# Norm roots on GpSimd, later GLA and MLA pieces, and keys and values loaded by block in a hybrid GLA/MLA layer

## The chip, the cores and the metric

The kernel runs on one core of one Trainium2 chip. The metric is the device time of one execution in microseconds (us), the median of several runs. The core has a tensor engine (PE, with its weight loads PEld), a vector engine (DVE), a scalar engine (ACT), a GpSimd engine (POOL) and a sync engine (SP) that here issues nearly all DMAs. Each engine runs its instructions in the order in which they stand in its queue.

## The reference, cut to what matters

One layer on x of shape (1, 2048, 1024) in float32:

```
n   = rms_norm(x, attn_norm);  z = n @ w_in     # split into gq gk gv g_low g_r c_q c_kv k_r
GLA: log_a = log_sigmoid(g_low @ w2 + b) / 16;  b = cumsum(log_a) in a chunk
     o_g   = chunked linear attention with exact pairwise decays (4 heads, 64 keys, 128 values)
     o_g   = rms_norm(o_g per head, gla_out_norm) * silu(g_r)
MLA: q = rms_norm(rms_norm(c_q) @ w_uq per head), k = rms_norm([rms_norm(c_kv) @ w_ukv, k_r] per head)
     rope on the last 32 of 96 dimensions;  o_m = block-causal softmax attention (8 heads)
h = x + concat(o_g, o_m) @ w_out
h = h + relu(rms_norm(h) @ w_up)^2 @ w_down
h = h + (p @ w_ple_proj) * sigmoid(rms_norm(h) @ w_ple_gate + b_ple_gate)
```

Every `rms_norm` needs the reciprocal root 1/sqrt(mean of squares + eps), one number a row (x, h), four a row (GLA heads) or eight a row (four query and four key heads).

## The kernel before

The work stands in three stages that follow each other.

The **first stage** (about 0 to 690 us) takes four blocks of 512 rows. For each block the rows of x are normed (`norm_rows`) and transposed into `nT`; then come the products with slices of `w_in`, each as three matmuls on a split into a high and a low part (`mm3`, lines 99 to 101): columns for c_q, g_low and k_r (304 wide), c_kv and a part of gv (320), gq and gk, the rest of gv (320), g_r (256). Each weight slice is split by ACT and DVE (lines 95, 96). Between these products two queues of small pieces are drained one by one by calls in the loops: `pend` holds the GLA pieces of the block before (`gla_pieces`: a diagonal, seven decay levels, the decays, two chunks, for each of two units of 256 rows), `mla_q` holds the MLA tiles (`mla_tile`: eight a block, each with its two products, norm, scaling, and a `store` that transposes q and k and writes them to DRAM). `later` holds a piece's second half back by one piece.

The **second stage** (to about 1260 us) is attention over eight heads and four query blocks; the last block's GLA pieces are drained inside it. The **third stage** (to the end) is the output product, the MLP and the gate, in two halves of 1024 rows; `rows_T` norms and transposes there.

The order on each engine is set by the framework's scheduler, which sorts the recorded instructions by priority (the order of the code) and its own cost estimates; loads of the activation table are put in afterwards where the functions demand them.

Lines that the prediction speaks of: `rstd_of` (106 to 115) makes the root: v on DVE (106), a first guess by an Exp on ACT (108), three Newton steps of three DVE instructions each (111, 112, 114). Line 428 transposes a GLA chunk's output `o`, which line 422 scales by the root; line 354 transposes the decayed keys `dk` (347). Lines 617 to 630 make the log decays `la` (Abs, Exp, Ln on ACT) and their running sums `bt` (matmul by a triangle, line 628). Line 384 is a level's score product, which needs `xq` and `dl` (377, 379) and those an Exp (368). Line 499 scales q by its root and gains, 501 and 503 scale k; line 511 transposes both. Line 740 sets a row of the key buffer `kT` to one. Line 921 transposes the normed h of the third stage.

Of the kernel before, what the change touches and what calls it, by code (L numbers as in the profile page):

```python
# [48 lines left out]
def hymba_block(ctx, tc, x, p, positions, attn_norm, w_in, gla_gate_w2, gla_gate_b,  # L49
# [53 lines left out]
    def rstd_of(ss, n, shape):  # L103

        v = small.tile(shape, F32, name="rs_v")
        V.tensor_scalar(out=v, in0=ss, scalar1=1.0 / n, scalar2=EPS, op0=ALU.mult, op1=ALU.add)
        y = small.tile(shape, F32, name="rs_y")
        A.activation(y, v.bitcast(I32), AF.Exp, bias=y0_b, scale=Y0_S)
        for _ in range(3):
            a = small.tile(shape, F32, name="rs_a")  # L110
            V.tensor_tensor(out=a, in0=y, in1=y, op=ALU.mult)  # L111
            V.scalar_tensor_tensor(out=a, in0=a, scalar=-0.5, in1=v, op0=ALU.mult, op1=ALU.mult)  # L112
            r = small.tile(shape, F32, name="rs_y")
            V.scalar_tensor_tensor(out=r, in0=a, scalar=1.5, in1=y, op0=ALU.add, op1=ALU.mult)  # L114
            y = r
        return y
# [120 lines left out]
    def gain_columns():  # L237
# [4 lines left out]
        V.tensor_scalar(out=gqk_b, in0=gqk_b, scalar1=1.0 / math.sqrt(QK), scalar2=None, op0=ALU.mult)  # L242
        V.tensor_tensor(out=gqk_b[:, 0:NOPE], in0=gqk_b[:, 0:NOPE], in1=gk_b, op=ALU.mult)
# [72 lines left out]
    LL, LC, EB, DP = 1, 1, 2, 3  # L316


    def gla_pieces(u, tok0, gq, gk, bt, gvs, gss):
# [17 lines left out]
        def decays():  # L337
            eb = gw.tile([P, 2, 2, P], F32, name="eb", bufs=EB)
# [4 lines left out]
            dk = tmp([P, 4, P], "dk")  # L343
            bc = bt.rearrange("p (a t) -> p a t", t=P)
            G.tensor_tensor(out=dk, in0=bc[:, :, P - 1:P].broadcast_to([P, 4, P]), in1=bc, op=ALU.subtract)
            A.activation(dk, dk, AF.Exp)
            G.tensor_tensor(out=dk, in0=gk.rearrange("p g (c t) -> p (g c) t", t=P), in1=dk, op=ALU.mult)
# [45 lines left out]
        def chunk(c):  # L393
# [15 lines left out]
            for g in range(2):  # L409
# [654 lines left out]
```

## Time and profile before

| | us |
|---|---|
| median of 3 runs (3119.1 to 3125.26) | 3120.78 |
| the profiled execution, its own time | 3113.97 |
| its span, first to last instruction | 3112.0 |
| PE busy in the span | 2982.2 |
| DVE busy | 1954.9 |
| ACT busy | 1251.7 |
| POOL busy | 202.9 |

The profiled execution took 6.8 us less than the median of the runs. An engine's busy time is the time in which it executed something; the waits of an engine are its idle times, put down to the instruction that ended them.

### The profile page before, as it was taken

Reading aid. Unit: us, or ns where it says so; the run is one execution under the profiler, and the core shown is the slowest. Engines: PE = TensorE matmul, PEld = TensorE weight load, DVE = VectorE, ACT = ScalarE, POOL = GpSimd, SP = SyncE. Lnnn points to the kernel's source line nnn. Section 1 sums busy time; section 2 is a strip of 40 time slices with the busy share of each in tenths; the row PEclk is TensorE's granted clock in tenths of the full one; section 3 lists DMA queues with packets and bytes.
Section 4 is the critical chain, followed back from the end, with each engine's and each line's share of the span. In section 5 each row is a group of like instructions: output and inputs, shape, how many; then the busy total and the mean of one; then the engine's idle time right before and its main releaser. Section 6 shows DMA issues by size and latency. Waiting matters only on the chain.

```text
span 3112.0 us, 41322 instructions
## 1 busy us (share of the span) xinstructions
PE 2982.2 (96%) x14851; PEld 2449.3 (79%) x14851; DVE 1954.9 (63%) x4389; ACT 1251.7 (40%) x2540; POOL 202.9 (7%) x408
## 2 busy tenths in 40 slices
PE   7899988887999999999999999999999999999999
PEld 6887878785677777788888888878888888888877
DVE  5979898887878787464444444464464444444463
ACT  7565665644666667432122221242232221222231
POOL 2322222321000000000000000000000000000000
PEclk9999999998999999999999999999999999999999
DMA  4535434352422320411111111113311111111111
GB/s 119 148 86 153 119 111 131 89 160 70 123 70 68 103 69 19 152 41 54 41 55 41 55 49 47 54 48 127 124 54 41 55 47 48 52 43 55 41 51 54
DMA packets 222525, 238.77 MB, mean 77 GB/s; under 512 B 26630, under 2 KB 174160, under 8 KB 220528
## 3 DMA queue, kind: packets, MB, share of 16 engines
q1 hardware_dynamic: 222000, 236.01, 25.9%
q8 instruction: 117, 1.92, 0.3%
q14 instruction: 88, 0.72, 0.1%
q0 software_dynamic: 320, 0.13, 0.0%
HBM read 185.60 MB, written 50.46 MB: 76 GB/s over the span
## 4 chain that ended last, share of the span: by engine, by line
PE 77%; DVE 15%; ACT 3%; issue 3%; DMA 2%; POOL 0%; SPq 0%; DVEq 0%; ACTq 0%; POOLq 0%
PE mm L101 10%; PE mm L100 10%; PE mm L99 10%; PE big L99 9%; PE big L100 9%; PE big L101 9%; PE mm L823 5%; PE tp L758 2%; PE big L797 2%; PE big L799 2%; PE big L798 2%; DVE w L96 2%; DVE rs_a L112 1%; DVE rs_a L111 1%; DVE rs_y L114 1%
## 5 line engine op out<-in xcount | busy, mean ns | idle before, releaser
L999 DVE TENSOR_TENSOR h<-big,h 128x1024 f32<-128x1024 f32 x256 | 313.1, 1223 | 265.1 <-PE big L101 264.9
L823 PE MATMUL mm<-ph,vv 128*66 128x512 f32 (+3 forms) x960 | 242.8, 366 | 3.4 <-ACT ph L92 2.6
L99 PE MATMUL mm<-w,nT 128*128 128x320 f32 (+2 forms) x640 | 204.3, 319 | 5.6 <-ACT w L95 2.8
L100 PE MATMUL mm<-w,nT 128*128 128x320 f32 (+2 forms) x640 | 199.4, 313 | 5.8 <-DVE w L96 5.1
L93 DVE TENSOR_TENSOR ph<-pe,ph 128x1024 fp32r<-128x1024 f32 (+4 forms) x224 | 176.6, 796 | 38.3 <-ACT ph L92 36.6
L101 PE MATMUL mm<-w,nT 128*128 128x320 f32 (+2 forms) x640 | 198.1, 311 | 1.7 <-DVE nT L93 1.7
L765 DVE TENSOR_REDUCE mx<-tp 128x1 f32<-128x512 f32 (+2 forms) x288 | 169.5, 606 | 14.5 <-PE tp L758 12.9
L823 PEld LDWEIGHTS mm<-ph,vv 128*66 128x66 f32 (+1 forms) x960 | 126.2, 138 | 56.1 <-ACT ph L92 4.4
L92 ACT CAST ph<-pe 128x1024 fp32r<-128x1024 f32 (+4 forms) x224 | 156.3, 712 | 28.7 <-PE mm L823 25.8
L99 PEld LDWEIGHTS mm<-w,nT 128*128 128x128 f32 x640 | 126.3, 197 | 10.3 <-ACT w L95 5.0
L100 PEld LDWEIGHTS mm<-w,nT 128*128 128x128 f32 x640 | 126.2, 198 | 9.2 <-DVE w L96 8.8
L758 PE MATMUL tp<-kT,qT 96*128 96x512 f32 (+2 forms) x320 | 125.3, 398 | 4.9 <-DVE mx L765 2.9
L101 PEld LDWEIGHTS mm<-w,nT 128*128 128x128 f32 x640 | 126.4, 198 | 4.3 <-DVE nT L93 2.4
L96 DVE SCALAR_TENSOR_TENSOR w<-raw,gain_a,w 128x256 fp32r<-128x256 f32 (+2 forms) x224 | 119.9, 548 | 10.3 <-ACT w L95 9.4
L797 PE MATMUL big<-qT,kT 97*128 97x512 f32 (+1 forms) x320 | 122.2, 382 | 2.2 <-ACT pe L810 1.3
L95 ACT ACTIVATE w<-raw,gain_a 128x256 fp32r<-128x256 f32 (+2 forms) x224 | 111.0, 533 | 31.8 <-DMA raw<-in_w_in_dram 15.6
L798 PE MATMUL big<-qT,kT 96*128 96x512 f32 (+1 forms) x320 | 119.8, 374 | 0.0
L799 PE MATMUL big<-qT,kT 96*128 96x512 f32 (+1 forms) x320 | 119.6, 374 | 0.0
L804 ACT ACTIVATE pe<-big 128x1024 f32<-128x1024 f32 x96 | 98.3, 1024 | 28.4 <-PE big L799 27.7
L758 PEld LDWEIGHTS tp<-kT,qT 96*128 96x128 f32 x320 | 61.2, 192 | 35.9 <-DVE mx L765 13.5
L810 ACT ACTIVATE pe<-big 128x512 f32<-128x512 f32 (+3 forms) x128 | 54.4, 437 | 65.2 <-DVE big L809 58.2
L797 PEld LDWEIGHTS big<-qT,kT 97*128 97x128 f32 x320 | 61.1, 191 | 21.6 <-ACT pe L810 6.7
(3372 smaller groups left out, 8166.2 us busy)
## 6 DMA issues: line engine op xcount, KB each, us to landing
raw<-in_w_mlp_up_dram SPq DMA_DIRECT2D x128, 256.0 KB, 2.8
raw<-in_w_mlp_down_dram SPq DMA_DIRECT2D x128, 256.0 KB, 3.0
raw<-in_w_in_dram SPq DMA_DIRECT2D x160, 128.0 KB, 2.5
qd<-qko SPq DMA_DIRECT2D x64, 192.0 KB, 2.7
kd<-qko SPq DMA_DIRECT2D x64, 192.0 KB, 2.9
kT<-kd SPq DMA_DIRECT2D x8, 1536.0 KB, 11.1
qT<-qd SPq DMA_DIRECT2D x32, 384.0 KB, 4.0
vd<-vt SPq DMA_DIRECT2D x32, 260.0 KB, 3.2
```

What stands on the lines that cost most here:

```text
L93: V.tensor_tensor(out=lo, in0=src, in1=hi, op=ALU.subtract)
L96: V.scalar_tensor_tensor(out=lo, in0=src, scalar=gain, in1=hi, op0=ALU.mult, op1=ALU.subtract)
L99: T.matmul(o, lhsT=a[0], rhs=b[0], start=first, stop=False)
L100: T.matmul(o, lhsT=a[0], rhs=b[1], start=False, stop=False)
L101: T.matmul(o, lhsT=a[1], rhs=b[0], start=False, stop=last)
L758: T.matmul(ps[:, :w_], lhsT=qT[0:QK, 0, s_ * P:(s_ + 1) * P], rhs=kT[0:QK, 0, c0:c0 + w_], start=True, stop=True)
L765: V.tensor_reduce(out=mx[:, a:a + 1], in_=ps[:, :w_], axis=AX.X, op=ALU.max)
L797: T.matmul(o, lhsT=kT[:, 0, ks], rhs=qT[:, 0, c0:], start=True, stop=False)
L798: T.matmul(o, lhsT=kT[0:QK, 0, ks], rhs=qT[0:QK, 1, c0:], start=False, stop=False)
L799: T.matmul(o, lhsT=kT[0:QK, 1, ks], rhs=qT[0:QK, 0, c0:], start=False, stop=True)
L823: T.matmul(po[0:vs.stop - vs.start, c0:], lhsT=vv[:, kb, vs], rhs=ph[:, l, e, c0:], start=(kb == 4 * jb and n_ == 0), stop=(lastk and n_ = ...
L999: V.tensor_tensor(out=hv, in0=ps, in1=hv, op=ALU.add)
```

## The change

The root is now two GpSimd instructions: v, and v to the power -0.5. The MLA tile's product of q with its gains moves to GpSimd, as does the product of the roots with the row roots; the scaling of q is one DVE instruction in place of four, and q's and k's scalings are issued at the next tile. The stores of a tile are issued after the next tile. A GLA chunk's squares and root stand ahead of its state update, and its output turn is issued with the next piece. The decays make `dk` first. The running sums are issued after the second and third tile of the following product. Keys and values are loaded 512 rows at a time, where they are first needed, and the row of ones is set by GpSimd. `gain_p` is padded.

```diff
+    mhalf = const.tile([P, 8], F32, name="mhalf")
+    V.memset(mhalf, -0.5)
...
-        V.tensor_scalar(out=v, in0=ss, scalar1=1.0 / n, scalar2=EPS, op0=ALU.mult, op1=ALU.add)
+        G.tensor_scalar(out=v, in0=ss, scalar1=1.0 / n, scalar2=EPS, op0=ALU.mult, op1=ALU.add)
         y = small.tile(shape, F32, name="rs_y")
-        A.activation(y, v.bitcast(I32), AF.Exp, bias=y0_b, scale=Y0_S)
-        for _ in range(3):
-            a = small.tile(shape, F32, name="rs_a")
-            V.tensor_tensor(out=a, in0=y, in1=y, op=ALU.mult)
-            V.scalar_tensor_tensor(out=a, in0=a, scalar=-0.5, in1=v, op0=ALU.mult, op1=ALU.mult)
-            r = small.tile(shape, F32, name="rs_y")
-            V.scalar_tensor_tensor(out=r, in0=a, scalar=1.5, in1=y, op0=ALU.add, op1=ALU.mult)
-            y = r
+        G.tensor_tensor(out=y, in0=v, in1=mhalf[:, :shape[1]], op=ALU.pow)
...
+    outs = []
...
+            dk = tmp([P, 4, P], "dk")
+            bc = bt.rearrange("p (a t) -> p a t", t=P)
+            G.tensor_tensor(out=dk, in0=bc[:, :, P - 1:P].broadcast_to([P, 4, P]), in1=bc, op=ALU.subtract)
+            A.activation(dk, dk, AF.Exp)
+            G.tensor_tensor(out=dk, in0=gk.rearrange("p g (c t) -> p (g c) t", t=P), in1=dk, op=ALU.mult)
             eb = gw.tile([P, 2, 2, P], F32, name="eb", bufs=EB)
...
+            for h in range(GH):
+                A.activation(junk, po[:, h], AF.Square, accum_out=ss[:, h:h + 1])
+            r = rstd_of(ss, GV, [P, GH])
             for g in range(2):
                 for j in range(2):
                     js = slice(j * 64, j * 64 + 64)
...
-            later(scale, LC)
+            outs.append(scale)
...
+        qno = qn[:, :, 0:NOPE]
+        G.tensor_tensor(out=qno, in0=qno, in1=gqk_b.unsqueeze(1).broadcast_to([P, 4, NOPE]), op=ALU.mult)
...
-        V.tensor_tensor(out=rn, in0=rs.rearrange("p (a h) -> p a h", h=4),
+        G.tensor_tensor(out=rn, in0=rs.rearrange("p (a h) -> p a h", h=4),
...
-        for hh in range(4):
-            V.scalar_tensor_tensor(out=qn[:, hh], in0=qn[:, hh], scalar=rn[:, 0, hh:hh + 1], in1=gqk_b,
-                                   op0=ALU.mult, op1=ALU.mult)
...
+        def scale():
+            V.tensor_tensor(out=qn, in0=qn, in1=rn[:, 0].unsqueeze(2).broadcast_to([P, 4, QK]), op=ALU.mult)
...
+        scales.append(scale)
         stores.append(store)
...
     def drain(n=1):
         for _ in range(n):
+            old, outs[:] = list(outs), []
             if pend:
                 pend.pop(0)()
                 if not pend:
                     later(None, 0)
+            for f in old:
+                f()
...
     def drain_mla(n=1):
         for _ in range(n):
+            old = list(stores)
+            while scales:
+                scales.pop(0)()
             if mla_q:
                 mla_q.pop(0)()
-            while len(stores) > (1 if mla_q else 0):
-                stores.pop(0)()
+            for f in old:
+                f()
+                stores.remove(f)
...
+        def running(la):
+            ps = ps_tp().rearrange("p (g c t) -> p g c t", g=2, c=2)
+            for c in range(2):
+                for g in range(2):
+                    T.matmul(ps[:, g, c], lhsT=la[:, c, g * P:(g + 1) * P], rhs=tri, start=True, stop=True)
...
+            sums.append(lambda la=la: running(la.rearrange("p (c f) -> p c f", c=2)))
...
             split(cT[:, 0, 2, ts_], cT[:, 1, 2, ts_], tp[:, 0])
+            if tt in (1, 2):
+                sums.pop(0)()
             drain(DY)
...
     def load_head(h):
         kT = ah.tile([QK + 1, 2, S], F32R, name="kT")
         vv = ah.tile([P, NT, VW], F32R, name="vv")
-        dma(out=kT[0:QK].bitcast(F32), in_=kd[h])
-        V.memset(kT[QK:QK + 1, 0].bitcast(F32), 1.0)
-        dma(out=vv.bitcast(F32), in_=vd[h])
+        G.memset(kT[QK:QK + 1, 0].bitcast(F32), 1.0)
         return kT, vv
...
+    def load_block(h, jb):
+        kT, vv = heads[h]
+        js, ks = slice(jb * BLK, (jb + 1) * BLK), slice(jb * 4, jb * 4 + 4)
+        dma(out=kT[0:QK, :, js].bitcast(F32), in_=kd[h, :, :, js])
+        dma(out=vv[:, ks].bitcast(F32), in_=vd[h, :, ks])
...
+            load_block(h, jb)
             qTs[n_], seq = shift_pieces(h, jb, heads[h][0])
```

What this moves, at three places. First PE in the second block, where the GLA chunk before is finished (`gv`, `st`, `sz`, `qe`: value and state products; `kdT`: state update; `o`: the output turn). Before:

```order
L402 MATMUL big<-gv,st_146 128x128
L403 MATMUL big<-sz_156,qe 128x128
L100 MATMUL mm<-w,nT_2309 128x304
...
L100 MATMUL mm<-w,nT_2309 128x304
L428 MATMUL tp<-ident,o_2687 128x128
L407 MATMUL tp<-gv,kdT 64x128
L428 MATMUL tp<-ident,o_2687 128x128
L407 MATMUL tp<-gv,kdT 64x128 x2
L428 MATMUL tp<-ident,o_2687 128x128
```

Now:

```order
L400 MATMUL tp<-gv,kdT 64x128 x4
L421 MATMUL tp<-ident,o_2401 128x128 x4
L98 MATMUL mm<-w,nT_2097 128x304
...
L100 MATMUL mm<-w,nT_2098 128x304
L629 MATMUL big<-w_124,lowT 128x256 x2
L608 MATMUL tp<-ident,c 128x128 x2
L609 MATMUL tp<-ident,c 17x128
L421 MATMUL tp<-ident,o_2479 128x128 x4
```

Before, seven matmuls of the product stood between a chunk's last state product and its output turn. Now each turn is one piece of four; the first stands after the next chunk's products, and 24 matmuls of the product stand between that and the second.

Second ACT in the same block, where `la` is made (`big` is the product with g_low, `dl` the first levels of the next unit). Before:

```order
L620 ACTIVATE la<-big 128x512 x2
L621 ACTIVATE la<-la 128x512 x2
L622 ACT_TABLE_LOAD
L622 ACTIVATE la<-la,ones_col 128x512 x2
L368 ACT_TABLE_LOAD
L368 ACTIVATE dl<-dl 128x512 x2
```

Now:

```order
L632 ACTIVATE la<-big 128x512
L634 ACT_TABLE_LOAD
L634 ACTIVATE la<-la,ones_col 128x512
L633 ACT_TABLE_LOAD
L633 ACTIVATE la<-la 128x512
L651 COPY ckv<-mm 128x128
L634 ACT_TABLE_LOAD
L634 ACTIVATE la<-la,ones_col 128x512
...
L361 ACT_TABLE_LOAD
L361 ACTIVATE dl<-dl 128x512 x3
```

Exp and Ln of the two units now alternate: four table loads where two stood, in each of the blocks two to four (the program has 19 loads in place of 13), and the levels' Exp comes behind the last.

Third POOL in an MLA tile of the last block (`qe` is a GLA piece's, the rest the tile's). Before:

```order
L341 TENSOR_TENSOR qe<-gq,eb 128x512
L475 TENSOR_TENSOR qa<-qn,rt_7330 128x128
L476 TENSOR_TENSOR qb<-qn,rt_7332 128x128
L477 TENSOR_TENSOR qn<-qa,qb 128x4x16
L478 TENSOR_TENSOR qn<-qa,qb 128x4x16
```

Now:

```order
L469 TENSOR_TENSOR qb<-qn,rt_6519 128x128
L473 TENSOR_TENSOR qn<-qn,gqk_b 128x4x64
L470 TENSOR_TENSOR qn<-qa,qb 128x4x16
L471 TENSOR_TENSOR qn<-qa,qb 128x4x16
L105 TENSOR_SCALAR rs_v<-ssq 128x8
L107 TENSOR_TENSOR rs_y<-rs_v,mhalf 128x8
L490 TENSOR_TENSOR rn<-rs_y,rc 128x8
```

The rotation's four instructions became eight with the gains, the root's two and the product of roots.

## Rows read from the trace of the kernel before

**Rows 1.** Windows by stage: busy us of each engine, granted clock, DMA share.

```profile
0.00:50.00 50.00, 31.40 (x185) 27.87 (x185) 32.75 (x126) 33.52 (x79) 20.80 (x65) 1.00 0.49 131
50.00:690.00 640.00, 575.44 (x3703) 516.71 (x3703) 546.82 (x1760) 382.29 (x1045) 169.60 (x326) 0.96 0.44 121
690.00:760.00 70.00, 50.09 (x229) 36.16 (x230) 52.88 (x140) 25.94 (x61) 12.48 (x17) 0.78 0.42 114
760.00:3112.00 2352.00, 2325.25 (x10736) 1868.59 (x10735) 1322.48 (x2367) 809.91 (x1357) 0.00 (x0) 1.00 0.21 62
```

The columns after the stretch and its length are PE, PEld, DVE, ACT and POOL (instructions in brackets), the granted clock, the DMA share and GB/s.

**Rows 2.** PE's waits from 50 to 690 us: total, times, longest.

```profile
PE tp L511 <- DVE qn L499: 20.3, 25, 2.3
PE tp L428 <- DVE o L422: 12.2, 9, 2.6
PE tp L354 <- POOL dk L347: 5.4, 3, 2.5
...
PE tp L511 <- DVE kn L501: 4.8, 8, 0.7
...
PE big L402 <- DVE st L386: 0.2, 1, 0.2
```

**Rows 3.** Windows of 4 us around one such wait, columns as in rows 1.

```profile
200.00:204.00 4.00, 1.97 (x14) 1.71 (x12) 3.76 (x9) 0.79 (x4) 3.32 (x5) 1.00 0.21 61
204.00:208.00 4.00, 3.43 (x11) 2.82 (x12) 1.25 (x5) 1.18 (x2) 1.17 (x2) 0.51 0.02 4
208.00:212.00 4.00, 4.00 (x14) 3.35 (x14) 0.00 (x0) 3.18 (x5) 1.09 (x2) 0.50 0.24 66
```

**Rows 4.** DVE groups up to 1300 us: busy us, mean ns, idle before.

```profile
L111 DVE TENSOR_TENSOR rs_a<-rs_y 128x8 f32<-128x8 f32 (+2 forms) x204 | 39.7, 194 | 7.7 <-ACT rs_y L108 5.3 <-DVE vt L480 0.2
L112 DVE SCALAR_TENSOR_TENSOR rs_a<-rs_a,rs_v 128x8 f32<-128x8 f32 (+2 forms) x204 | 39.6, 194 | 3.4
L499 DVE SCALAR_TENSOR_TENSOR qn<-qn,rn,gqk_b 128x96 f32<-128x96 f32 x128 | 39.2, 367 | 0.0
L114 DVE SCALAR_TENSOR_TENSOR rs_y<-rs_a,rs_y 128x8 f32<-128x8 f32 (+2 forms) x204 | 36.0, 177 | 3.7
L501 DVE TENSOR_TENSOR kn<-kn,rn 128x256 f32<-128x256 f32 x32 | 18.5, 577 | 0.0
L740 DVE MEMSET kT<- 1x2048 f32 x8 | 14.1, 1765 | 4.8 <-issue 2.9 <-PE mm L101 1.4 <-PE big L798 0.5
```

**Rows 5.** Timeline around 306 us, DVE and POOL: start, duration.

```profile
306.47 0.16 DVE L112 SCALAR_TENSOR_TENSOR rs_a<-rs_a,rs_v 128x8 f32<-128x8 f32 x1
...
306.94 1.26 POOL L347 TENSOR_TENSOR dk<-gk,dk 128x512 f32<-128x512 f32 x1 [5.33 <-ACT dk L346]
307.06 1.17 DVE L112 SCALAR_TENSOR_TENSOR rs_a<-rs_a,rs_v 128x8 f32<-128x8 f32 x1
```

**Rows 6.** POOL groups of the whole span, columns as in rows 4.

```profile
L366 POOL TENSOR_TENSOR dl<-bt 128x256 f32<-128x256 f32 x56 | 38.7, 692 | 63.9 <-PE tp L428 17.5 <-PE tp L628 16.0 <-PE big L330 14.7
...
L341 POOL TENSOR_TENSOR qe<-gq,eb 128x512 f32<-128x512 f32 x8 | 10.6, 1326 | 99.0 <-ACT gq L677 98.8
...
L603 POOL TENSOR_TENSOR krr<-kra,krb 128x16 f32<-128x16 f32 x16 | 3.6, 223 | 0.0
```

**Rows 7.** ACT groups up to 1300 us, columns as in rows 4.

```profile
L108 ACT ACTIVATE rs_y<-rs_v,y_b 128x8 f32<-128x8 int32 (+2 forms) x68 | 20.5, 301 | 26.9 <-DVE rs_v L106 26.6
...
L622 ACT ACT_TABLE_LOAD x5 | 6.4, 1283 | 0.1
L622 ACT ACTIVATE la<-la,ones_col 128x512 f32<-128x512 f32 x8 | 5.4, 716 | 0.1
```

**Rows 8.** PE's waits from 690 to 1260 us, columns as in rows 2.

```profile
PE tp L428 <- DVE o L422: 9.4, 3, 6.3
PE big L384 <- DVE dl L379: 3.6, 1, 3.6
```

**Rows 9.** PE's waits from 1250 us to the end, the longest row.

```profile
PE tp L921 <- DVE nrm L125: 5.0, 2, 2.5
```

More of the change, by code (lines that the diff above doesn't have):

```diff
@@ L222, in hymba_block @@
     cst = ca.tile([P, NT, 2, NF], F32, name="cst")
-    gqk_b = ca.tile([P, QK], F32, name="gqk_b")
-    V.memset(gqk_b[:, NOPE:], 1.0)
-    G.dma_start(out=gqk_b[:, 0:NOPE], in_=qk_norm_q[0, 0:NOPE].partition_broadcast(P))
+    gqk_b = ca.tile([P, NOPE], F32, name="gqk_b")
+    G.dma_start(out=gqk_b, in_=qk_norm_q[0, 0:NOPE].partition_broadcast(P))
     gk_b = tmp([P, NOPE], "gk_b")
@@ L241, in gain_columns @@
         V.tensor_scalar(out=cols[:, 3:4], in0=cols[:, 3:4], scalar1=0.5, scalar2=None, op0=ALU.mult)
-        V.tensor_scalar(out=gqk_b, in0=gqk_b, scalar1=1.0 / math.sqrt(QK), scalar2=None, op0=ALU.mult)
-        V.tensor_tensor(out=gqk_b[:, 0:NOPE], in0=gqk_b[:, 0:NOPE], in1=gk_b, op=ALU.mult)
+        for t_ in (gqk_b, rope_g[0]):
+            V.tensor_scalar(out=t_, in0=t_, scalar1=1.0 / math.sqrt(QK), scalar2=None, op0=ALU.mult)
+        V.tensor_tensor(out=gqk_b, in0=gqk_b, in1=gk_b, op=ALU.mult)
     def rope_tables():
@@ L408, in chunk @@
                          start=True, stop=True)
+            ss = small.tile([P, GH], F32, name="oss")
+            junk = gw.tile([P, GV], BF16, name="junk", tag="tmp", bufs=TMP)
+            for h in range(GH):
+                A.activation(junk, po[:, h], AF.Square, accum_out=ss[:, h:h + 1])
+            r = rstd_of(ss, GV, [P, GH])
             for g in range(2):
@@ L413, in chunk @@
                                            in1=pk[js, g], op0=ALU.mult, op1=ALU.add)
-            ss = small.tile([P, GH], F32, name="oss")
-            junk = gw.tile([P, GV], BF16, name="junk", tag="tmp", bufs=TMP)
-            for h in range(GH):
-                A.activation(junk, po[:, h], AF.Square, accum_out=ss[:, h:h + 1])
-            r = rstd_of(ss, GV, [P, GH])
             o1 = tmp([P, GH, GV], "o1")
@@ L610, in hymba_block @@
             drain(DX)
-        bts = []
+        bts, sums = [], []
+        def running(la):
[3 more added lines that the diff above has]
+                    T.matmul(ps[:, g, c], lhsT=la[:, c, g * P:(g + 1) * P], rhs=tri, start=True, stop=True)
+            bt = gin.tile([P, 512], F32, name="bt")
+            A.copy(out=bt, in_=ps.rearrange("p g c t -> p (g c t)"))
+            bts.append(bt)
         for u in range(2):
@@ L623, in hymba_block @@
             V.scalar_tensor_tensor(out=la, in0=ps, scalar=0.0, in1=la, op0=ALU.min, op1=ALU.subtract)
-            la = la.rearrange("p (c f) -> p c f", c=2)
-            ps = ps_tp().rearrange("p (g c t) -> p g c t", g=2, c=2)
-            for c in range(2):
-                for g in range(2):
-                    T.matmul(ps[:, g, c], lhsT=la[:, c, g * P:(g + 1) * P], rhs=tri, start=True, stop=True)
-            bt = gin.tile([P, 512], F32, name="bt")
-            A.copy(out=bt, in_=ps.rearrange("p g c t -> p (g c t)"))
-            bts.append(bt)
+            sums.append(lambda la=la: running(la.rearrange("p (c f) -> p c f", c=2)))
         if b == 0:
@@ L712, in hymba_block @@
                 drain_mla(DM[f * 4 + tt])
-    drain_mla(len(mla_q))
+    drain_mla(len(mla_q) + 2)
     drain(4)
@@ L897, in hymba_block @@
             built[n_] = None
-        if pgl is not None and not pend:
+        if pgl is not None and not pend and not outs:
             pgl.close()
```

22 lines of the change are left out of this document (7 added, 15 removed).

## The prediction

> **What bounds the kernel now.** I read the windows by stage first. From 760 us on PE is busy 2325 of 2352 us at full clock [rows 1]: there only what shortens PE's own work would count, and the change gives PE the same matmuls. From 50 to 690 us PE is busy 575.4 of 640, so it stands idle for 64.6 us, and its granted clock is 0.96; DVE is busy 546.8 there, the other engines far less. From 690 to 760 us PE stands idle for 19.9 us at a clock of 0.78. The gain, if there is one, lies in these two stretches.
>
> PE's own waits say for whom [rows 2]. The answer has 16 rows, which add up to 62.2 us; DVE's scaling of q and k before line 511 ends 20.3 + 4.8 = 25.1, the GLA output's scaling before line 428 12.2, GpSimd's decayed keys before line 354 5.4, and the other 12 rows together 19.5. One such wait in windows of 4 us shows what else it costs [rows 3]: from 200 to 204 PE works 1.97 of 4 us while DVE works 3.76; then the clock is 0.51 and 0.50 for the next 8 us, that is the lower level of 1.2 GHz, though PE is busy nearly all of that time. A clock of 0.96 over 640 us is 25.6 us of full clock lost, 0.78 over 70 us another 15.4.
>
> **The change, part by part.** DVE first. The Newton steps cost 39.7 + 39.6 + 36.0 = 115.3 us in the first stage [rows 4], three times three instructions for each of 68 roots. The four scalings of q cost 39.2; one instruction over 384 elements replaces them, which I bound by one and one and a half of the 256-element product of k (577 ns), 18 to 28 us for 32 tiles: 11 to 21 saved. So DVE falls from 547 to about 415 of 640 us. ACT loses 68 guesses, 20.5 us [rows 7]. Part of DVE's time was GpSimd's doing: the same Newton instruction takes 0.16 us alone and 1.17 us where it begins 0.12 us behind a GpSimd product of 1.26 us, and ends with it [rows 5]. Roots on GpSimd can't be held up that way.
>
> What GpSimd gets: for each of 68 roots two instructions, for each of 32 tiles a 128x256 product (692 ns) and a product of eight elements. No row shows a power. The nearest rows are products on GpSimd, 223 ns for 16 elements and 1326 ns for 512 [rows 6]; I take 0.3 us for v and 0.5 for the power, nearer to the small shape, as a tile has one to eight elements a row, and keep both ends. That is 54 + 32 x (0.69 + 0.25) = 84 us on top of 170 in 640: far from a bound. A root as a chain was 0.3 + 9 x 0.19 = 2.0 us of execution [rows 4, 7] and becomes 0.8 (bounds 0.45 and 2.65).
>
> Now PE's waits, gain minus, loss plus.
> - Line 511, 25.1 us: scaling is issued a tile earlier than the transposes, with nine matmuls and at least one product piece between them, on a DVE that has a quarter more room. I leave 5: -20 (bounds -12, half, and -25).
> - Line 428, 12.2 us: 24 matmuls stand between a chunk's products and its output turn in place of seven. At 575.44 / 3703 = 0.155 us a matmul [rows 1] that is 3.7 us in place of 1.1. Leave 5: -7 (0 to -12).
> - Line 354, 5.4 us: dk is made first, its turn stands behind two tiles: -5 (0 to -5).
> - A new wait. In blocks two to four the table loads between the last Abs and the next level's Exp are four in place of two, 1283 ns each [rows 7]. Those levels' score products stand 55 matmuls, 8.5 us, behind the start of the c_kv product. ACT's row of work up to that Exp is four loads (5.1 us), five activations of some 0.7 (3.5) and about 1.5 of copies between, and DVE then makes xq and dl (three instructions of about 0.45, by the width between a Newton step and the k product): 11.5 us. PE is 3 us early: +9 for three blocks (0 to +18). What is late next is the running sums behind that product, which have a whole tile to spare.
> - The other twelve rows, 19.5 us, are mostly DVE's late splits: -8 (-3 to -13).
> - The clock, 25.6 us: the stretch around the new wait keeps its low clock, other stalls over 2 us go: -10 (0 to -20).
> - 690 to 760 us: line 428 waits 9.4 us there and line 384 3.6 [rows 8]. The two chunks' squares now stand together and the roots leave DVE, and the 1.77 us of the key row's memset [rows 4] leave DVE too, for GpSimd, where the root is queued behind it; the turns still wait for the scaling. -9 with the clock (-3 to -20).
> - More GpSimd time beside DVE's remaining two-input instructions: +4 (0 to +20).
> - Third stage: line 921 waits 5.0 us, twice the last norm [rows 9]; the root's chain is 1.2 us shorter: -2 (+3 to -5).
> - The start, 0 to 50 us: PE is idle for 18.6 us [rows 1]. The first root now queues behind GpSimd's own DMA issues and memsets, while DVE is freed: 0 (4 either way).
> - Keys and values by block: 0. The cover is that PE, when attention opens, waits for the output turns and not for keys [rows 8], and later works 99% of the time; if that cover went, a later first key block would cost what it is late. The gain excludes itself likewise. The pad of gain_p: 0, nothing reads it.
>
> The sum is -20 - 7 - 5 + 9 - 8 - 10 - 9 + 4 - 2 = -48 us. On the profiled execution that is 3113.97 - 48 = 3066; the median of the runs is 6.8 above that execution, so 3120.8 - 48 = **3073**.
>
> Two rules of the Trainium skill bear on this. "ScalarE: Activation LUTs", section "What ACT_TABLE_LOAD costs", gives a load 1283 ns and a drain of about 1380 beside it, 2.66 us for each switch; the trace agrees on the load and shows 0.1 us idle in all before the five loads and before the eight Ln [rows 7]. By the rows the six added loads are 7.7 us of ACT, by the page an estimated 16, which would make the new wait +17 and the sum -40. "SBUF — State Buffer", section "Who interferes with whom", says that a DVE instruction with two SBUF inputs and a GpSimd instruction that reads SBUF exclude each other for a whole instruction; rows 5 agree.
>
> **The rivals.** *The power is slow (slower).* GpSimd's power could be a software routine of many steps. Each of the 16 chunk outputs holds PE until its root is there; beyond 0.8 us for a root every further us costs 16 us, so the gain of 48 is gone at 3.8 us a root, three times the dearest GpSimd row. At 5 us: 3120.8 - 48 + 16 x 4.2 = 3140. For it: no row shows a power. Against: one to eight elements a row.
> *GpSimd's added time and the table loads eat half.* If DVE is held up for all 84 us that GpSimd gains, DVE comes to 415 + 84 = 499 of 640, and its waits shrink by a third of what I took; with the new wait at its bound the sum is about -23: 3098. For it: rows 5. Against: the tiny instructions that were held up most are gone.
> *PE becomes the bound.* If DVE was the only brake, 50 of the 64.6 us, 20 of the lost clock and 5 of the second stretch come back, 75 us: 3046. For it: where PE stalls, DVE is full [rows 3]. Against: the table loads.
> *The waits only change their names*: what PE waits for next (ACT's copies, the weights' split) ends as late; 3121.
>
> **How the numbers follow.** Chances: forecast (3058 to 3087) 0.53, half eaten 0.18, PE bound 0.14, no change 0.05, slow power 0.10. A measurement of this kernel tells about 0.2%, 6 us, from no change. Faster: 0.53 + 0.18 + 0.14 = 0.85, less a little for the half-eaten case at its worst, 0.84; same 0.05; slower 0.11. The range leaves out the slow power and the ends of the others: 3040 to 3106.
>
> **What would show it.** Right: from 50 to 690 us in the changed profile the same work ends some 35 to 40 us earlier, DVE busy is about 130 us less, the waits of the transposes of q, k and the outputs are under 12 us together, and a score product waits about 3 us behind the table loads in three blocks. The power's row says at once whether 0.5 us holds. Wrong: a power of over 2 us, PE waits on GpSimd roots, a clock under 0.96 in the first stage, or idle PE after 760 us over the 26.8 us of now.

## The result and the profile after

The changed kernel takes 3101.45 us (median of four runs, 3101.0 to 3102.7), the kernel before 3119.94 beside it; the ratio is 0.9944, 95% interval 0.9931 to 0.9956. It is faster by 18.5 us where 48 were forecast. The profiled execution has a span of 3099.3 us at a granted clock of 0.984.

The windows by stage, columns as in [rows 1]:

```profile
0.00:50.00 50.00, 30.23 (x188) 26.16 (x188) 25.91 (x89) 37.05 (x80) 24.54 (x75) 1.00 0.48 133
50.00:690.00 640.00, 565.88 (x3686) 515.30 (x3687) 466.20 (x1026) 374.63 (x985) 291.01 (x506) 0.96 0.43 120
690.00:760.00 70.00, 55.78 (x233) 40.87 (x232) 46.52 (x114) 26.33 (x58) 20.06 (x25) 0.68 0.49 119
760.00:3099.00 2339.00, 2317.49 (x10749) 1868.77 (x10747) 1270.06 (x2026) 806.17 (x1325) 40.11 (x74) 1.00 0.21 63
```

DVE lost 81 us of work between 50 and 690 us, not 130, and POOL gained 121, not 84. PE does no more in that stretch than before (3686 matmuls against 3703) and the clock there is the same 0.96. So the first stage is no shorter. Three products mark the stages: the last one of the MLA pieces, the first of the third stage and the last of the kernel. First the kernel before, then the changed one (timeline: start, duration):

```profile
670.99 0.39 PE L101 MATMUL mm<-wkv,cT 128*128 128x512 f32 x1
1266.97 0.48 PE L99 MATMUL mm<-w__15434,xT 128*128 128x512 f32 x1
3105.48 0.39 PE L101 MATMUL big<-w__27876,a 128*128 128x512 f32 x1
```

```profile
674.84 0.39 PE L100 MATMUL mm<-wkv,cT 128*128 128x512 f32 x1
1265.08 0.48 PE L98 MATMUL mm<-w__14398,xT 128*128 128x512 f32 x1
3092.82 0.39 PE L100 MATMUL big<-w__26360,a 128*128 128x512 f32 x1
```

The first stage is 3.9 us longer, the attention (the differences of these starts) 590.2 against 596.0, the third stage 1827.7 against 1838.5. The whole gain of this execution lies behind 690 us, and most of it where almost nothing was forecast.

PE's waits from 50 to 690 us, as in [rows 2]:

```profile
PE mm L98 <- ACT qn L461: 18.1, 9, 3.8
PE tp L505 <- DVE qn L494: 12.3, 8, 2.5
PE mm L98 <- DVE gs L716: 8.9, 13, 1.5
PE mm L98 <- ACT nT L91: 8.4, 3, 3.3
PE tp L505 <- DVE kn L497: 6.0, 7, 0.9
PE big L377 <- DVE dl L372: 5.9, 6, 1.5
PE big L377 <- DVE xq L370: 4.8, 3, 1.6
...
PE tp L421 <- DVE o L415: 1.5, 3, 0.5
```

The transposes of q and k (now line 505) wait 18.3 us, before 25.1; the output turns (421) 1.5, before 12.2; the decayed keys are gone from the list. In their place stands a wait that hardly existed: the next product (L98) waits 18.1 us until ACT has copied q out of PSUM (before, 1.2). GpSimd's power, by form (columns as in [rows 6]):

```profile
L107 POOL TENSOR_TENSOR rs_y<-rs_v,mhalf 128x8 f32<-128x8 f32 x36 | 59.4, 1650 | 3.0
...
L107 POOL TENSOR_TENSOR rs_y<-rs_v,mhalf 128x1 f32<-128x1 f32 x48 | 27.6, 577 | 3.5 <-POOL rs_v L105 0.2
...
L107 POOL TENSOR_TENSOR rs_y<-rs_v,mhalf 128x4 f32<-128x4 f32 x16 | 16.2, 1013 | 1.4 <-POOL rs_v L105 0.2
```

A power of eight elements a row takes 1650 ns, over three times the 0.5 us that was taken; one of one element 577. Who waits for it is the longest of DVE's waits from 50 to 690 us (total, times, longest):

```profile
DVE qn L494 <- POOL rn L490: 62.8, 32, 3.2
DVE w L95 <- ACT w L94: 18.0, 28, 1.7
```

That is 1.96 us a tile. The old chain's nine DVE instructions took about 1.7 us together, but DVE did not stand still between them. Here are two of them in the kernel before, with a weight split in between, which starts before the instruction ahead of it has ended (timeline: start, duration):

```profile
471.36 0.15 DVE L111 TENSOR_TENSOR rs_a<-rs_y 128x8 f32<-128x8 f32 x1
471.43 0.48 DVE L96 SCALAR_TENSOR_TENSOR w<-raw,gain_a,w 128x256 fp32r<-128x256 f32 x1
471.83 0.16 DVE L112 SCALAR_TENSOR_TENSOR rs_a<-rs_a,rs_v 128x8 f32<-128x8 f32 x1
```

Now DVE's 466 us of work and these 63 of waiting make 529 of 640, where its work alone was 547 before: most of what DVE was relieved of has become a wait at the scaling of q. One tile shows a way from there to PE (timeline around 470 us: start, duration, in brackets the idle time before and its end):

```profile
469.83 0.20 POOL L105 TENSOR_SCALAR rs_v<-ssq 128x8 f32<-128x8 f32 x1
470.11 1.65 POOL L107 TENSOR_TENSOR rs_y<-rs_v,mhalf 128x8 f32<-128x8 f32 x1
471.84 0.20 POOL L490 TENSOR_TENSOR rn<-rs_y,rc 128x8 f32<-128x8 f32 x1
472.08 0.56 DVE L494 TENSOR_TENSOR qn<-qn,rn 128x384 f32<-128x384 f32 x1 [2.48 <-POOL rn L490]
...
473.09 2.06 DVE L95 SCALAR_TENSOR_TENSOR w<-raw,gain_a,w 128x256 fp32r<-128x256 f32 x5
473.60 4.48 SPq L167 DMA_DIRECT2D raw<-in_w_in_dram  x7
...
476.70 0.51 ACT L94 ACTIVATE w<-raw,gain_a 128x256 fp32r<-128x256 f32 x1 [4.87 <-DMA raw<-in_w_in_dram]
...
477.49 0.47 ACT L461 COPY qn<-mm 128x384 f32<-128x384 f32 x1
478.01 0.58 PE L98 MATMUL mm<-w,nT 128*128 128x256 f32 x1 [3.79 <-ACT qn L461]
```

DVE stands for 2.48 us at the scaling of q, and the weight splits behind it (L95) start late. They free the buffers of the raw weights, so SP's next loads start at 473.60. ACT, which works in order, waits 4.87 us for one of them, and q's copy is queued behind; the next product waits for that copy, so PE stands still for 3.79 us. This is the longest of nine such waits; that the other eight came about in the same way is not shown. Over the stage ACT's waits for raw weights of `w_in` are 37.7 us, before 15.6; its waits for GpSimd's decay differences 25.0, in the version with the eights back (below) 9.6:

```profile
ACT w L94 <- DMA raw<-in_w_in_dram: 37.7, 19, 4.9
ACT dl L361 <- POOL dl L360: 25.0, 17, 3.6
```

### The profile page after: what moved, and what is told of

The parts are those of the page before. It is cut to its first block, busy times and chain, and to the rows that moved or that the text cites. A ratio compares the mean times of both kernels' runs of the same rounds, so it can differ in the third digit from the quotient of the medians.

```text
span 3099.3 us, 40489 instructions
## 1 busy us (share of the span) xinstructions
PE 2969.4 (96%) x14851; PEld 2451.1 (79%) x14851; DVE 1808.7 (58%) x3253; ACT 1244.2 (40%) x2446; POOL 375.7 (12%) x680
## 4 chain that ended last, share of the span: by engine, by line
issue 54%; PE 30%; DVE 5%; POOL 5%; ACT 4%; DMA 2%; SPq 1%; DVEq 0%; POOLq 0%; ACTq 0%
PE mm L834 5%; PE mm L98 3%; PE mm L100 3%; PE mm L99 3%; PE tp L769 2%; PE big L808 2%; PE big L810 2%; PE big L809 2%; POOL rs_y L107 2%; PE big L100 1%; PE big L98 1%; PE big L99 1%; PE big L377 1%; DMA raw<-in_w_in_dram 1%; DVE xq L370 1%
## 5 line engine op out<-in xcount | busy, mean ns | idle before, releaser
L105 POOL TENSOR_SCALAR rs_v<-nss 128x1 f32<-128x1 f32 x48 | 11.9, 249 | 1873.9 <-ACT nsq L113 1867.5
L98 PE MATMUL mm<-w,nT 128*128 128x320 f32 (+2 forms) x640 | 205.2, 321 | 29.0 <-ACT qn L461 17.9
L92 DVE TENSOR_TENSOR ph<-pe,ph 128x1024 fp32r<-128x1024 f32 (+3 forms) x224 | 177.5, 799 | 49.4 <-ACT ph L91 46.8
L91 ACT CAST ph<-pe 128x1024 fp32r<-128x1024 f32 (+3 forms) x224 | 156.9, 711 | 31.4 <-PE mm L834 28.0
L98 PEld LDWEIGHTS mm<-w,nT 128*128 128x128 f32 x640 | 128.4, 201 | 35.3 <-ACT qn L461 19.8
L95 DVE SCALAR_TENSOR_TENSOR w<-raw,gain_a,w 128x256 fp32r<-128x256 f32 (+2 forms) x224 | 122.7, 586 | 28.8 <-ACT w L94 26.5
L99 PEld LDWEIGHTS mm<-w,nT 128*128 128x128 f32 x640 | 128.5, 201 | 2.0 <-DVE w L95 1.3
L100 PEld LDWEIGHTS mm<-w,nT 128*128 128x128 f32 x640 | 128.3, 200 | 0.0
L107 POOL TENSOR_TENSOR rs_y<-rs_v,mhalf 128x1 f32<-128x1 f32 (+2 forms) x100 | 103.1, 1033 | 7.9 <-POOL rs_v L105 0.3
L769 PEld LDWEIGHTS tp<-kT,qT 96*128 96x128 f32 x320 | 62.5, 196 | 35.5 <-DVE mx L776 13.4
```

The source lines that it names most:

```text
L92: V.tensor_tensor(out=lo, in0=src, in1=hi, op=ALU.subtract)
L98: T.matmul(o, lhsT=a[0], rhs=b[0], start=first, stop=False)
L99: T.matmul(o, lhsT=a[0], rhs=b[1], start=False, stop=False)
L100: T.matmul(o, lhsT=a[1], rhs=b[0], start=False, stop=last)
L107: G.tensor_tensor(out=y, in0=v, in1=mhalf[:, :shape[1]], op=ALU.pow)
L769: T.matmul(ps[:, :w_], lhsT=qT[0:QK, 0, s_ * P:(s_ + 1) * P], rhs=kT[0:QK, 0, c0:c0 + w_], start=True, stop=True)
```

## The experiments

Each median is of four or more runs (of this kernel, in microseconds), the ratio is to the kernel before on the same chip with its 95% interval; the stages are the differences between the three products above, from one profiled execution each, so they need not add up to the medians.

| run | median | ratio to before | first stage | attention | third stage |
|---|---|---|---|---|---|
| before | 3119.94 | | 671.0 | 596.0 | 1838.5 |
| the change | 3101.45 | 0.9944 (0.9931 to 0.9956) | 674.8 | 590.2 | 1827.7 |
| e1_all_roots | 3164.24 | 1.0143 (1.0128 to 1.0159) | 688.7 | 598.2 | 1869.4 |
| e2_narrow_roots | 3141.63 | 1.0079 (1.0064 to 1.0094) | 659.4 | 596.2 | 1877.2 |
| e3_orders_only | 3136.14 | 1.0055 (1.0042 to 1.0068) | 651.9 | 592.8 | 1888.8 |
| e4_exp_ln_grouped | 3100.23 | 0.9940 (0.9927 to 0.9952) | 675.3 | 588.7 | 1827.4 |
| e7_all_roots_w2_back | 3121.25 | 1.0000 (0.9991 to 1.0009) | 684.9 | 600.3 | 1826.6 |
| e9_orders_only_w2_back | 3089.91 | 0.9898 (0.9884 to 0.9912) | 653.9 | 587.2 | 1840.2 |
| e10_orders_narrow_roots | 3075.34 | 0.9851 (0.9837 to 0.9866) | 647.5 | 587.2 | 1828.8 |
| e11_gain_p_16 | 3141.91 | 1.0067 (1.0049 to 1.0085) | 676.4 | 588.4 | 1869.6 |
| e12_wide8_back | 3074.66 | 0.9851 (0.9838 to 0.9865) | 649.1 | 590.2 | 1828.1 |
| e13_wide4_back | 3104.50 | 0.9949 (0.9936 to 0.9961) | 678.4 | 592.1 | 1828.4 |
| e14_multiply_for_power8 | 3069.52 | 0.9836 (0.9822 to 0.9849) | 643.2 | 589.1 | 1829.0 |
| e15_narrow_grouped | 3075.17 | 0.9849 (0.9835 to 0.9863) | 646.9 | 592.4 | 1827.6 |
| e16_gain_p_112 | 3100.93 | 0.9936 (0.9921 to 0.9951) | 674.4 | 583.7 | 1828.9 |
| e17_mla_order_back | 3074.47 | 0.9853 (0.9837 to 0.9870) | 652.7 | 589.2 | 1828.2 |
| e18_outs_back | 3082.02 | 0.9875 (0.9859 to 0.9890) | 650.3 | 595.4 | 1827.6 |
| e19_sums_back | 3074.30 | 0.9853 (0.9838 to 0.9868) | 643.6 | 590.4 | 1829.0 |
| e20_gain_on_vector | 3077.58 | 0.9871 (0.9857 to 0.9886) | 652.1 | 589.5 | 1829.7 |
| e22_whole_head_loads | 3076.63 | 0.9869 (0.9852 to 0.9885) | 647.5 | 593.3 | 1825.8 |

**Roots against orders.** My first theory was that the roots decide only the third stage. Three kernels take the change apart: the kernel before with the new root, the same for roots of one element alone, and the changed kernel with the old root.

```diff
 # e1_all_roots: the kernel before with
-        A.activation(y, v.bitcast(I32), AF.Exp, bias=y0_b, scale=Y0_S)
...
+        G.tensor_scalar(out=v, in0=ss, scalar1=1.0 / n, scalar2=EPS, op0=ALU.mult, op1=ALU.add)
+        G.tensor_tensor(out=y, in0=v, in1=mhalf[:, :shape[1]], op=ALU.pow)
 # e2_narrow_roots: the same under
+        if shape[1] == 1:
 # e3_orders_only: the changed kernel with the old rstd_of
```

> The kernel before with all roots on GpSimd (v and power), every order of work as before. Theory A (the power by width decides: 577 ns for one element a row, 1013 for four, 1650 for eight; a root of eight takes as long as the chain on VectorE, one of one element half): the first stage gains nothing, the norms at the gates of the third stage give 10 us, so 13 us faster than before (8 to 18). Rival B (GpSimd's roots hold the first stage up and hide what the new orders gain): no faster than before, 0 to 5 us. Rival C (the new orders cost, the roots gain): 25 us or more faster than before.

> The kernel before with only the roots of one element a row on GpSimd (48 of 100), those of four and eight on VectorE and ScalarE as before. A: 10 to 14 us faster than before, as much as with all roots. B: clearly faster than with all roots, by 10 us or more, since the wide ones are the costly ones. C: clearly less than with all roots, since the wide roots bring a part of the gain.

> The changed kernel with the old root (VectorE and the Exp of ScalarE), all its new orders kept. A: 5 us faster than before (0 to 8), since the new orders give little and the gate norms lose their 10 us. B: 30 us or more faster than before, well under the changed kernel's time. C: slower than before, by up to 10 us.

None of the theories foresaw that both halves are slower than before, by 45 and 17 us, and together faster by 18.5. The stages tell why. In the first stage the new root costs 17.7 us in the old order (688.7 against 671.0) and 22.9 in the new (674.8 against 651.9), while the narrow ones alone gain 11.6: theory A falls, B holds for the wide roots. But the third stage, whose code is the same, takes 31 to 50 us more in all three. PE's waits do not explain it: PE is busy nearly all the time. Windows of the same 800 us in the third stage, first of the kernel before, then of a later run (e11 below) with `w2` where e1 has it:

```profile
2100.00:2900.00 800.00, 799.02 (x3554) 661.09 (x3554) 389.73 (x550) 194.27 (x332) 0.00 (x0) 1.00 0.20 64
```

```profile
2100.00:2900.00 800.00, 799.16 (x3471) 646.91 (x3470) 367.88 (x462) 188.67 (x319) 7.07 (x16) 1.00 0.21 63
```

At the same clock and the same busy share PE starts 3471 matmuls in place of 3554. What differs is where the tiles `w2`, which hold the third stage's weights, lie in SBUF (`raw2` and `bias_p` shift along with them, but no matmul reads those): in the program as built they begin at byte 35296 before and after the change, at 35168 in e1, 35328 in e2 and 35424 in e3, since the four scratch buffers `rs_a` of 32 bytes and the constants had gone or come. The change itself loses the 128 bytes of `rs_a`, and its 128 bytes of `gain_p` put them back.

**The addresses held fast.** Four kernels: e1 and e3 with `w2` at 35296 again, a version with only the narrow roots on GpSimd, and the changed kernel without its padding.

```diff
 # e7_all_roots_w2_back: e1 with       gain_p = gain_cols(cc, "gain_p", ple_norm[0], 8, 48)
 # e9_orders_only_w2_back: e3 with     gain_p = gain_cols(cc, "gain_p", ple_norm[0], 8, 16)
 # e10_orders_narrow_roots: the changed kernel, in rstd_of
+        if shape[1] == 1:            # the power on GpSimd; else the old root
 # e11_gain_p_16: the changed kernel with
-                gain_p = gain_cols(cc, "gain_p", ple_norm[0], 8, 48)
+                gain_p = gain_cols(cc, "gain_p", ple_norm[0], 8, 16)
```

> The kernel before with all roots on GpSimd, as in the run with all roots, but with gain_p 48 columns wide, so that the third stage's weight tiles w2 stand where they stand in the kernel before (the root's four scratch buffers, that are gone, had moved them by 128 bytes; in that run the matmuls of the third stage followed one another every 232 ns, before every 227). Theory D (those addresses, not the roots, slow the third stage): the third stage is 10 us shorter than before, the first stage ends 9 us later (as in the run with all roots), in all within 8 us of before. Rival E (the roots themselves slow the third stage): 45 us slower than before, as in the run with all roots.

> The changed kernel with the old root on VectorE and ScalarE, all new orders kept, and gain_p 16 columns wide, which puts w2 where it stands in the kernel before. D: the first stage ends 19 us earlier than before (as in the run with the orders alone), the third stage is as before, so 25 us faster than before (15 to 35), and faster than the changed kernel. E: 17 us slower than before, as in the run with the orders alone.

> The changed kernel with the power only where a root has one element a row (577 ns), and the old root for four and eight (1013 and 1650 ns on GpSimd); w2 where it stands before (gain_p 16 wide). Theory F (the wide powers stand in the chain of the first stage and eat what the new orders gain): the first stage ends 30 us earlier than before, the gate norms give 10 us, 40 us faster than before (30 to 48), 20 us faster than the changed kernel. Rival G (the new waits behind ScalarE's copies and table loads eat it, whatever the root): no faster than the changed kernel.

> The changed kernel with gain_p 16 columns wide instead of 48, nothing else: w2 stands 128 bytes lower. D: first stage as in the changed kernel, third stage 45 us longer, 30 us slower than before. E: no difference to the changed kernel.

D holds in e7, e9 and e11: with `w2` back all roots on GpSimd are worth nothing (1.0000), the orders alone 31 us, and the padding taken away costs the changed kernel 40 us; its third stage alone is 42 us longer. E falls. F holds: with only the narrow roots on GpSimd the time is 3075.34, 45.5 under before and within 3 us of the forecast for the whole change. G falls.

**Which width, and length or place.** The power of four elements apart from that of eight, and a multiplication in the place of the power of eight.

```diff
 # e12_wide8_back: the changed kernel, old root for eight, gain_p 16 wide
+        if shape[1] < 8:             # the power on GpSimd; else the old root
 # e13_wide4_back: old root for four, gain_p 8 wide (w2 at the same address)
+        if shape[1] != 4:            # the power on GpSimd; else the old root
 # e14_multiply_for_power8: the changed kernel with
-        G.tensor_tensor(out=y, in0=v, in1=mhalf[:, :shape[1]], op=ALU.pow)
+        G.tensor_tensor(out=y, in0=v, in1=mhalf[:, :shape[1]], op=ALU.pow if shape[1] < 8 else ALU.mult)
```

> The changed kernel with only the roots of eight elements back on VectorE and ScalarE (36 of 100), those of one and of four on GpSimd; w2 where it stands before. Theory F8 (the eights are what holds the first stage: rn is ready late and 62.8 us of VectorE's idle time stand ahead of the scaling of q): 40 us faster than before or more (36 to 48), within 8 us of the version that keeps only the narrow roots on GpSimd. Rival (any power on GpSimd costs by its time, 59 us for the eights and 16 for the fours): about 38 us, 6 us or more short of that version.

> The changed kernel with only the roots of four elements (16 of 100, GLA's output norm) back on VectorE and ScalarE, those of one and eight on GpSimd; w2 where it stands before. F8: as the changed kernel, 19 us faster than before (15 to 25). Rival: 25 us or more.

> The changed kernel with a multiplication in the place of the power of eight elements, so the roots of the MLA norms are not computed; same queue, same neighbours, about 0.2 us for 1.65 us. If the length of the power is what costs (36 by 1.45 us, 52 us less on GpSimd): 42 us faster than before or more. If it is the place (the root stands behind the rotary and gain products in GpSimd's queue, 2.5 us a piece, and VectorE waits for it): no more than 30 us faster than before.

F8 holds on both sides: taking the 36 eights back gives 27 us over the change, taking the 16 fours back nothing measurable (though in e13 six table loads go with them, see below). And it is the length: the same queue, neighbours and waits with a short instruction in the power's place give 3069.52. Every SBUF tile of e14 lies where it lies in the changed kernel, so addresses play no part in this; in e9, e10, e12, e13 and the kernels built on them many tiles of the first stage lie 128 or 160 bytes further on, and no run shows what that alone is worth. In e14 DVE's wait for `rn` and PE's for q's copy shrink by about half or more, and ACT's for the decay differences only from 25.0 to 20.3, so that one is hardly what costs. One row each of DVE, ACT and PE from 50 to 690 us:

```profile
DVE qn L494 <- POOL rn L490: 23.6, 15, 2.8
ACT dl L361 <- POOL dl L360: 20.3, 22, 2.8
PE mm L98 <- ACT qn L461: 9.3, 9, 1.5
```

In e12 PE's wait for q's copy and both of ACT's waits shrink as well, while PE's waits for the scaling of q and for `dl` grow (12.3 to 15.0, 5.9 to 9.4); PE, then ACT, from 50 to 690 us:

```profile
PE tp L520 <- DVE qn L509: 15.0, 16, 1.4
PE big L392 <- DVE dl L387: 9.4, 7, 3.4
...
PE mm L100 <- ACT qn L476: 5.1, 5, 1.3
```

```profile
ACT w L96 <- DMA raw<-in_w_in_dram: 23.0, 18, 2.9
...
ACT dl L376 <- POOL dl L375: 9.6, 12, 2.8
```

In e12 it is GpSimd, not DVE, that waits at this place: 85.5 us before `rn` for DVE's last Newton step, while DVE waits 1.6 for `rn`.

**The table loads.** In the code of these two kernels each block has Abs and Exp of both units first, then both Ln.

```diff
+            las.append((la, ps))
+        for la, ps in las:
             A.activation(la, la, AF.Ln, bias=ones_col)
```

> The changed kernel with Abs and Exp of both units first and then both Ln, which takes two table loads out of each block. If the loads ahead of the score products' inputs (14.1 us of waits for dl and xq) are paid by the end, 8 to 10 us faster than the changed kernel; if what ends the first stage is the chain of the MLA pieces and GLA pieces elsewhere, within 3 us of it.

> The version with only the narrow roots on GpSimd (45 us faster than before), with Abs and Exp of both units ahead of both Ln in each block, which takes table loads away. If the wait of the score products for dl (8.2 us there) now counts, since the wide roots no longer hide it: 3 to 8 us faster still, 49 to 53 us under before; if not, the same 45 us.

The times are the same (1.2 and 0.2 us apart), but they say nothing of the loads, for neither edit took any away: in e4 the scheduler issued the old order again, and e10, on which e15 is built, already had both Exps ahead of both Lns. ACT in e4's second block (start, duration):

```profile
201.52 1.28 ACT L636 ACT_TABLE_LOAD   x1
202.81 0.72 ACT L636 ACTIVATE la<-la,ones_col 128x512 f32<-128x512 f32 x1
203.56 1.28 ACT L633 ACT_TABLE_LOAD   x1
204.85 0.63 ACT L633 ACTIVATE la<-la 128x512 f32<-128x512 f32 x1
```

e4 has 19 loads, like the changed kernel; e15 has 13, like e10. What does bear on them: every run with the fours on GpSimd has 19 loads, in the old orders too (e1, e7), and every run with the fours on the old root has 13, in the new orders too (e9). So e13 has six loads fewer than the change, and e10 six fewer than e12, and neither pair differs by more than some 3 us. But the loads and the fours go together there, and one could hide the other.

**The orders one by one**, each taken back in e12:

```diff
 # e17_mla_order_back
-        scales.append(scale)
+        scale()
...
-            for f in old:
-                f()
-                stores.remove(f)
+            while len(stores) > (1 if mla_q else 0):
+                stores.pop(0)()
 # e18_outs_back
-            outs.append(scale)
+            later(scale, LL)
 # e19_sums_back
-            sums.append(lambda la=la: running(la.rearrange("p (c f) -> p c f", c=2)))
+            running(la.rearrange("p (c f) -> p c f", c=2))
...
-            if tt in (1, 2):
-                sums.pop(0)()
 # e20_gain_on_vector: four scalings of q with gqk_b on VectorE, no product on GpSimd
 # e22_whole_head_loads: load_block's two loads for the whole head, in load_head
```

> The version with the eights back on VectorE (47 us faster than before), with the MLA scalings issued at once and the transposes one piece later, as in the kernel before; the gain product stays on GpSimd. The prediction's term for this order is 20 us of waits for qn: by it 27 us faster than before. If the other new orders carry the gain (GLA's output turns 7, dk first 5, sums, block loads): 40 us or more faster than before.

> The version with the eights back on VectorE, with GLA's output turns issued one piece later as in the kernel before, not one drain later. The prediction's term is 7 us: 40 us faster than before. If the term was too small, and the turns are what holds up: 30 us or less.

> The version with the eights back on VectorE, with the running sums issued at once, between the two units, as in the kernel before. The prediction has their late issue as a new wait of 9 us for the score products behind table loads, against some 4 us of waits that go: by it 5 us faster than that version. If the late sums are a gain of their own (TensorE no longer waits for la): 5 to 10 us slower than it.

> The version with the eights back on VectorE, with q's gain on VectorE again: four scalings of 96 elements with the gain instead of one of 384, no gain product on GpSimd. VectorE then has 0.44 us more a piece (1.23 us a piece in the kernel before against 0.79 with one scaling), 14 us in all, and GpSimd 26 us less. If the shorter scaling carries the first stage's gain: 10 to 20 us slower than that version (28 to 38 us faster than before). If it is hidden beside TensorE: within 4 us of that version.

> The version with the eights back on VectorE, with keys and values loaded a whole head at a time, as before. The prediction's term is 0. If the blocks open the attention earlier (35 us from the last MLA product to the first strip against 42 before): 5 to 8 us slower than that version; if the start waits for something else: within 3 us.

By the medians the MLA order is worth 0, the late sums 0, the gain product 2.9, the block loads 2.0 and the output turns 7.4; by the ratios, each against the kernel before on its own chip, 1, 1, 6, 6 and 7. The intervals are 4 to 5 us wide on either side, so of these only the turns stand out; of their gain 5.2 us lie in the attention (595.4 against 590.2) and 1.2 in the first stage (650.3 against 649.1). The MLA order surely isn't worth the 20 us of its term. With the old MLA order PE waits 24.4 us for q and 4.8 for k, with the new one 15.0 and 5.9, and the time is the same: 8 us of waiting less did not make the kernel shorter.

```profile
PE tp L520 <- DVE qn L509: 24.4, 20, 2.2
...
PE tp L520 <- DVE kn L512: 4.8, 8, 0.8
```

**The address once more:**

```diff
 # e16_gain_p_112: the changed kernel with
+                gain_p = gain_cols(cc, "gain_p", ple_norm[0], 8, 112)
```

> The changed kernel with gain_p 112 columns wide: w2 stands 256 bytes higher, in the run with 16 columns 128 bytes lower (its third stage was 42 us longer). If the offset within 256 bytes is what counts: as the changed kernel, matmuls 227 ns apart. If the offset within 512 bytes against xT and a: the third stage is longer by 30 us or more again.

At 256 bytes more (35552) the third stage takes 1828.9 us, as at 35296: the offset within 256 bytes fits all five addresses tried. It is 224 at the two fast ones, as for `xT` and `a`, the tiles that `w2` is multiplied with, and 96, 0 and 96 at the slow ones.

## Why the prediction was wrong

- **The step that failed** is "I take 0.3 us for v and 0.5 for the power, nearer to the small shape", and with it that a root's time was counted as GpSimd's load alone. v takes 0.20 to 0.25 us. The power takes 577, 1013 and 1650 ns for one, four and eight elements a row, some 0.15 us for each further element on 0.43. A root of eight, 1.85 us, lay inside the stated bounds of a root (0.45 to 2.65), though the power by itself is longer than the dearest row that the bounds came from (1.33); the sum used 0.8, near the low end, and carried no bounds for it. GpSimd gained 121 us in the first stage, not 84.
- **What hung on it.** The price was laid on the wrong roots. The rival of the slow power counted 16 chunk outputs, 16 us for every further us; those fours cost nothing measurable (e13 against the change, e12 against e10). The 36 eights went into GpSimd's load, "far from a bound". But DVE, which works in order, waits for 32 of them at the scaling of q, 62.8 us in all, and no term of the sum stands for that wait. e12 and e14 show the cost: 27 to 32 us.
- **DVE's room of 130 us**, from which most other terms were argued, did not come: 81 us of work less, 63 of waiting more. It was counted too large in any case. DVE's instructions overlap, as the three rows of the kernel before show in the section on the result, and the prediction took whole durations from a busy time: the groups' own busy times between 50 and 690 us add up to 629 before and 509 after, 120 less.
- **Line 511, -20:** wrong by itself too. The wait fell from 25.1 to 18.3 us in the change and to 20.9 in e12, and taking the order back there costs nothing (e17).
- **Line 428, -7:** the wait fell by more, from 12.2 to 1.5 us. That taking the order back costs 7.4 (e18) fits the term by luck: only 1.2 of it lie in the first stage, for which the term stood. **Line 354, -5:** the wait is gone; its worth alone was not tried.
- **The new wait, +9:** it came, 10.7 us at the score products (line 377). What it is worth is not shown: e4 and e15 moved no table load, and in e19, with the sums issued at once and the time the same, PE waits 5.8 us there and 5.0 for `la`. No drain shows beside the 1283 ns of a load: in the rows of e4 above, Ln starts 0.01 us behind its load.
- **The other twelve rows, -8:** wrong. PE's rows apart from those named so far add up to 42.7 us in the change, before 19.5; the wait for q's copy is 18.1 of them.
- **The clock, -10:** none in the change, 0.96 as before. Without the long power it is the larger part of what the first stage gains. PE from 50 us to the end of the first stage, in the kernel before, the change, e12 and e14 (length, PE busy and its matmuls, granted clock, DMA share, GB/s):

```profile
50.00:671.00 621.00, 558.47 (x3568) 0.96 0.44 121
50.00:675.00 625.00, 550.99 (x3562) 0.96 0.43 120
50.00:649.00 599.00, 537.97 (x3564) 0.99 0.46 126
50.00:643.00 593.00, 535.28 (x3566) 0.99 0.47 127
```

  The matmuls are the same within six. Against the kernel before, PE's busy time is 20.5 us less in e12 and 23.2 in e14, at the higher clock; its idle time, 62.5 us before, is 61.0 and 57.7. By the clocks alone (0.04 of 621 us lost before, 0.01 of 599 in e12) I estimate 19 us. So the waits that the sum named got shorter, but PE's idle time as a whole hardly did (in the change it rose to 74.0). The sum had it the other way round: 31 us from PE's waits, 10 from the clock.
- **690 to 760 us, -9:** the attention with its opening is 5.8 us shorter, inside the bounds, though the granted clock there is 0.68 (before 0.78).
- **Contention, +4:** not shown apart; what can be read lies inside the bounds (0 to +20). DVE's weight split takes 590 ns on average from 50 to 690 us, before 547 and in e12 547: 9 us for 208 of them. The scaling of k's sum of squares (line 486) takes 565, before 340: 7 us for 32. The Trainium skill, "SBUF — State Buffer", section "Who interferes with whom", says that a DVE instruction with two SBUF inputs contends with a GpSimd instruction that reads SBUF; the split has two such inputs, and its longer durations fit that.
- **Third stage, -2:** too small by 9 us. The norm's wait fell as forecast, from 5.0 to 1.2, but with it go the other stalls at the two gates and the lower clock there (from 2050 to 2100 us PE works 48.7 us at a clock of 1.00, before 45.6 at 0.97); the narrow roots give 11 us (1838.5 to 1827.7; with the old root, e9, 1840.2).
- **"The pad of gain_p: 0, nothing reads it":** wrong. It is worth 40 us (e11): it undoes what the loss of four scratch buffers does to the address of `w2`.
- **The rivals.** "Eats half" named 3098, the nearest time. Its owner was another: not execution held up and not the table loads, but a wait in DVE's queue, so the near number is luck. It had 0.18. "The waits only change their names" named ACT's copies, and PE's wait for q's copy did grow from 1.2 to 18.1 us; its 3121 misses what is gained behind the first stage.
- **Luck in the total.** e10 and e12 come within 3 us of the forecast 3073, and e14 within 4. But with the wide power out of the way the first stage gives 22 to 28 us, not 37, and most of that through the clock; the third stage gives 10, not 2.

Left open: the orders give 31 us (e9), and those taken back one by one own 12 of them by the medians, some 21 by the ratios; the rest is either shared between them or lies in `dk` being made first or in the squares standing ahead of the state update, which no run took back alone.

e12 and e10 beat both kernels. e12's median is 46.8 us under that of the kernel before on the same chip (3121.46), e10's 45.5 under its own (3120.81); both are 26 to 27 us under the change.

## What to carry to other kernels

Moving a chain to an idle engine doesn't free the engine that left it, if that one must wait for the answer in order: compare the chain's old work with the new wait, by shape, before counting room, and take no sum of overlapping durations from a busy time. Price an operation that no row shows at both ends and lay each end on every place that uses it, the widest first. Look in the trace whether an edit moved what it was to move before reading its time. And when a constant or a scratch buffer comes or goes, look first whether a stage with unchanged code still starts as many matmuls in the same time.

## What the runs showed of the hardware that was not expected

- The rate of unchanged matmuls hung on the address of the tiles that hold their weights. With `w2` at 35296 or 35552 bytes PE started 3554 or 3553 matmuls from 2100 to 2900 us, at 35168 it started 3471, both at a clock of 1.00; at 35328 and 35424 the third stage was 48 us longer than with the same roots at 35296 (e2 against e10, e3 against e9). `xT` and `a` kept their addresses, and the fast addresses of `w2` are those that lie at the same offset within 256 bytes as they do. Why is not shown.
- GpSimd's power grows steeply with the elements of a row: 577, 1013 and 1650 ns for one, four and eight, while v over the same shapes takes 249, 203 and 198.
